# Tying the modulation products and the scan's result transposes to the program's order in a two-block network

## The chip, the cores and the metric

The kernel runs on one core of one Trainium2 chip. Its time is the device time of one execution in microseconds; the time shown for a kernel is the median of several executions. The trace belongs to one further execution, taken with the hardware profiler.

TensorE (PE in the profile; its weight loads are PEld) does the matrix products, VectorE (DVE), ScalarE (ACT) and GpSimd (POOL) the elementwise work, and SyncE's queue (SP) issues the DMA transfers. Each engine works through its own list of instructions in order; semaphores hold an instruction until its operands are there.

## The reference

Two blocks of two layers each, on 256 positions ("lat") and 256 context positions ("ctx") of width 2048, all in fp32. The layers are sliding-window attention, latent attention (mla), a layer with a pooling half and a recurrent half (RWKV), and grouped attention. Ahead of each layer the inputs are modulated by vectors that come from a condition and a large weight matrix (2048 x 6144 per layer). Cut to the modulation and the recurrent half of the third layer:

```python
shift_l, scale_l, gate_l = split(silu(c) @ mod_w[l] + mod_b[l], 3)
shift_c, scale_c, gate_c = split(silu(c_ctx) @ mod_w[l] + mod_b[l], 3)
hl, hc = xl * (1 + scale_l) + shift_l, xc * (1 + scale_c) + shift_c
...
def step(S, xs):                    # per head, along the sequence, both directions
    r, w, k, v, a, b = xs
    sa = einsum('bhvk,bhk->bhv', S, a)
    S = S * w + outer(sa, b) + outer(v, k)
    return S, einsum('bhvk,bhk->bhv', S, r)
...
yn = ((y - mean(y)) * rsqrt(var(y) + GN_EPS)) * gn_g + gn_b
out = (concat([pool(al), yn + bonus]) * silu(gate)) @ ev_w_out
```

## The kernel before

**Products and weights.** All weights come from device memory as fp32 and are used once. `weights` issues the DMA into a tile `raw` on SyncE's queue; `split` turns it into a high part `whi` (ScalarE, L339) and a low part `wlo` (VectorE, L340), so each block of a projection is three products on TensorE (L368 to L370, output `a`). After each block `fill` runs so many steps of side work as the stage's rate says.

**Stages.** First projections (to 157 us of the trace), sliding-window attention (to 705), first out projection (to 885), mla (to 1320), second out projection (to 1450), the third layer with pooling and recurrence (to 2605), third out projection (to 2780), grouped attention and its out projection.

**Modulation.** `mod_steps` is a generator of side work: each step takes one loaded tile `mraw` (1 MB, 192 loads in all; some are halves of another layout, `mod_h`) and issues its matrix products `mv` (L270), four to a step, side by side in four column groups, at the end of which the result is turned and added to `mod`. `PACE` gives the steps per block of weights for each stage: 0.3, 0.5, 0.2, 0, 0.25, 0.5 for the two attention stages, the out projections and the third layer, in the order of the program; the first projections run at rate 0 and demand their groups by `need`. `mod_open` gives a stage buffers for `mraw`, and `mod_close` uses up what is loaded. In the second out projection the rate is 0, but `mod_open` with three buffers lets one load go out.

**Order.** The code is traced, and a scheduler then places the instructions of each engine by priority and by a model of when operands are ready. So an instruction may stand earlier or later on its engine than the code issued it. `keep_in_program_order` ties an instruction behind the one that the code issued just before it on the same engine. Before the change, the second to fourth product of a modulation step are tied; the first, raised in priority, goes where the scheduler's model has it ready.

**The scan.** The recurrence is done in 16 units (8 groups of heads by two directions), each in eight steps. A step is four or five products into a tile `chain` (L1434, L1438, L1444, L1448, L1457) that hang on each other through copies: `Rp` (VectorE, L1437), `SV` (VectorE and ScalarE, L1445, L1446, L1454), `y` (ScalarE, L1460). After the last step y is normalized (VectorE L1465 to L1476, with a Square on ScalarE and a power on GpSimd), and turned by eight transposes `yt` in two banks of four (L1487). Beside a unit's steps the next unit's inputs are made ready: small triangular inversions (`inv`, `z`, `x`, `Z`; L1396 to L1420), Gram matrices (`gram`, L1286), and the projections of the layer itself go on as products `a`.

## Time and profile before

| what | value |
|---|---|
| median of 3 executions | 3263.63 us (3262.27 to 3267.89) |
| profiled execution | 3252.14 us, its span 3250.0 us |
| mean granted TensorE clock (1 is 2.4 GHz) | 0.981 |
| TensorE products / weight loads busy | 95% / 74% of the span |
| VectorE / ScalarE / GpSimd busy | 65% / 46% / 11% |
| read from device memory | 517.46 MB, 170 GB/s with the writes |

The busy share of TensorE counts pipelined products from start to modelled end; the granted clock says in which of two levels the engine ran, 1.00 (2.4 GHz) or 0.50 (1.2 GHz). The profiled execution is shorter than the three that were timed.

### The profile page before, as it was taken

The numbers are of one execution on the slowest core, as the hardware profiler recorded it, in microseconds if no ns is written. First come the engines' busy times: TensorE is split into PE (matmuls) and PEld (weight loads), VectorE is DVE, ScalarE is ACT, GpSimd is POOL, SyncE is SP. The second block draws the span as 40 slices with busy tenths as digits, with TensorE's granted clock in tenths as the row PEclk, the third lists the DMA queues.
The fourth block names the chain that finished last, engine by engine and source line by source line (L and its number), as shares of the span: only waits on it lengthen the run. The fifth ranks groups of instructions, "written<-read, shape, count | busy, mean of one in ns | idle before, by whom it ended". The sixth has DMA issues, their size and how long they took to land. (4 is left out here: it accounts for less than half of the span.)

```text
span 3250.0 us, 53765 instructions
## 1 busy us (share of the span) xinstructions
PE 3080.6 (95%) x20018; PEld 2399.4 (74%) x20018; DVE 2101.4 (65%) x4663; ACT 1481.1 (46%) x3237; POOL 347.7 (11%) x536
## 2 busy tenths in 40 slices
PE   6999999989988999999999999999999999899997
PEld 4667777767777878897776666766767768678887
DVE  3356455543476666665887788778877555857766
ACT  3324444442376666653334333433434424646664
POOL 0000000000001111000122222222221101200000
PEclk8999999999999999999999999999999999999999
DMA  8843444358654656766434434334445474443454
GB/s 309 319 158 130 149 139 153 137 185 283 232 168 136 229 195 230 258 224 204 142 95 150 127 110 133 98 105 148 124 130 161 165 269 141 161 143 130 143 180 152
DMA packets 270773, 556.10 MB, mean 171 GB/s; under 512 B 122928, under 2 KB 150704, under 8 KB 244912
## 3 DMA queue, kind: packets, MB, share of 16 engines
q1 hardware_dynamic: 270512, 552.68, 51.0%
q8 instruction: 157, 2.57, 0.3%
q14 instruction: 104, 0.85, 0.1%
HBM read 517.46 MB, written 35.13 MB: 170 GB/s over the span
## 5 line engine op out<-in xcount | busy, mean ns | idle before, releaser
L340 DVE TENSOR_TENSOR wlo<-raw,whi 128x512 fp32r<-128x512 f32 (+2 forms) x1000 | 660.5, 668 | 545.7 <-ACT whi L339 510.8
L368 PE MATMUL a<-hhi,whi 128*128 128x512 f32 (+1 forms) x2752 | 972.4, 354 | 16.6 <-ACT whi L339 12.1
L339 ACT CAST whi<-raw 128x512 fp32r<-128x512 f32 (+2 forms) x1000 | 592.7, 599 | 800.9 <-PE a L369 467.5
L369 PE MATMUL a<-hlo,whi 128*128 128x512 f32 (+1 forms) x2752 | 947.2, 345 | 0.3 <-DVE hlo L461 0.3
L370 PE MATMUL a<-hhi,wlo 128*128 128x512 f32 (+1 forms) x2752 | 939.8, 347 | 3.4 <-DVE wlo L340 3.1
L368 PEld LDWEIGHTS a<-hhi,whi 128*128 128x128 f32 x2752 | 524.9, 191 | 124.1 <-ACT whi L339 43.3
L370 PEld LDWEIGHTS a<-hhi,wlo 128*128 128x128 f32 x2752 | 522.1, 191 | 61.7 <-DVE wlo L340 8.4
L369 PEld LDWEIGHTS a<-hlo,whi 128*128 128x128 f32 x2752 | 525.6, 191 | 48.7 <-issue 4.5
L472 POOL TENSOR_TENSOR rs<-st,mhalf 128x4 f32<-128x4 f32 (+3 forms) x109 | 149.0, 1367 | 1660.8 <-DVE st L469 1632.9
L368 PE MATMUL a<-whi,hhi 128*128 128x512 f32 (+1 forms) x672 | 262.3, 401 | 15.9 <-ACT sq L629 6.4
L369 PE MATMUL a<-wlo,hhi 128*128 128x512 f32 (+1 forms) x672 | 264.6, 394 | 1.5 <-DVE wlo L340 1.3
L370 PE MATMUL a<-whi,hlo 128*128 128x512 f32 (+1 forms) x672 | 261.2, 391 | 0.0
L270 PE MATMUL mv<-mraw,cs 128*32 128x512 f32 (+1 forms) x1792 | 212.3, 562 | 16.2 <-DMA mraw<-mod_w 10.9
L1443 POOL TENSOR_SCALAR SD<-SV,DL 64x64 f32<-64x64 f32 x224 | 123.8, 553 | 462.5 <-DVE SV L1454 446.2
L368 PEld LDWEIGHTS a<-whi,hhi 128*128 128x128 f32 x672 | 127.1, 191 | 61.5 <-ACT whi L339 12.8
L369 PEld LDWEIGHTS a<-wlo,hhi 128*128 128x128 f32 x672 | 128.9, 192 | 33.7 <-DVE wlo L340 7.7
L370 PEld LDWEIGHTS a<-whi,hlo 128*128 128x128 f32 x672 | 128.5, 191 | 27.5 <-issue 2.9
L581 ACT ACTIVATE pr<-sc,nm 128x512 f32<-128x512 f32 (+1 forms) x128 | 81.0, 633 | 91.9 <-DVE nm L578 66.4
L1437 DVE COPY Rp<-chain 64x64 f32<-64x64 f32 x256 | 56.7, 221 | 72.1 <-PE chain L1434 69.1
L572 DVE TENSOR_REDUCE mx<-sc 128x1 f32<-128x512 f32 (+1 forms) x128 | 78.9, 617 | 37.1 <-PE sc L782 16.1
L1460 ACT COPY y<-chain 64x64 f32<-64x64 f32 x256 | 52.7, 206 | 109.1 <-PE chain L1457 98.4
L1446 ACT COPY SV<-chain 64x64 f32<-64x64 f32 x128 | 26.5, 207 | 161.5 <-DVE SV L1445 153.5
(379 smaller groups left out, 4678.9 us busy)
## 6 DMA issues: line engine op xcount, KB each, us to landing
mraw<-mod_w SPq DMA_DIRECT2D x160, 1024.0 KB, 4.9
raw<-od_in SPq DMA_DIRECT2D x88, 512.0 KB, 3.6
raw<-swa_in SPq DMA_DIRECT2D x72, 512.0 KB, 3.5
mraw<-mod_h SPq DMA_DIRECT2D x32, 1024.0 KB, 6.1
raw<-ev_rkv SPq DMA_DIRECT2D x64, 384.0 KB, 4.0
raw<-ev_in SPq DMA_DIRECT2D x48, 512.0 KB, 4.0
raw<-swa_out SPq DMA_DIRECT2D x40, 512.0 KB, 5.6
raw<-ev_out SPq DMA_DIRECT2D x40, 512.0 KB, 3.7
```

Source lines behind the costliest of these rows:

```text
L270: mm = nc.tensor.matmul(pb[32 * j : 32 * j + 32, :cols], cs[:, 32 * k + 30 - 2 * n : 32 * k + 62 - 2 * n], raw[:, kk, :], start=(n == 0 an ...
L339: nc.scalar.copy(whi, raw)
L340: nc.vector.tensor_tensor(wlo, raw, whi.bitcast(F32), op=ALU.subtract)
L368: mm(out, ah, bh, start=first, stop=False, skip_group_check=shared)
L369: mm(out, ah, bl, start=False, stop=False, skip_group_check=shared)
L370: mm(out, al, bh, start=False, stop=last, skip_group_check=shared)
L472: self.nc.gpsimd.tensor_tensor(dst, stv, mv, op=ALU.pow)
L572: nc.vector.reduce_max(mx, sc, axis=AX.X)
L581: nc.scalar.activation(pr[:, :n], sc, AF.Exp, scale=scale, bias=nm, accum_out=sm)
L1437: nc.vector.tensor_copy(Rp[half[hh]], blk(0, hh))
L1443: nc.gpsimd.tensor_scalar(SD[r_], SV[r_, hh, c, :], DL[r_, c : c + 1], None, ALU.mult)
L1460: nc.scalar.copy(y[r_, c, :], blk(3 * P, hh))
```

## The change

Three edits. In `mod_steps` the first product of a step is tied to the program's order too wherever the stage's rate is above 0 (`paced`). In `rwkv` the first transpose of each bank of four is tied. In the second out projection `mod_open` and `mod_close` are gone, so that this stage has no `mraw` buffers, and the one load that it issued is issued in the next stage.

```diff
--- before.py
+++ after.py
@@ -264,6 +264,7 @@
                             self.mod_load()
                         raw = self.mod_ahead.pop(0)
 
+                        paced = "mod" in self.side and self.side["mod"][1] > 0
                         for kk in range(nk):
                             k, j = nk * q + kk, kk % 4
                             with self.tc.high_priority(None if kk else 0):
@@ -272,7 +273,7 @@
                                     raw[:, kk, :], start=(n == 0 and k < 4), stop=(n == len(gs) - 1 and k >= KD - 4),
                                     tile_position=(0, 32 * j),
                                 )
-                                if kk:
+                                if kk or paced:
                                     self.tc.keep_in_program_order(mm)
                         self.mod_wait = MOD_LAG
                         yield
@@ -1484,7 +1485,9 @@
             for n in range(4):
                 c = 2 * n + c0
                 src = y[:, c : c + 2, :].rearrange("p c t -> p (c t)") if c < NCH - 1 else yw
-                nc.tensor.transpose(pb[:, n * P : (n + 1) * P], src, self.ident)
+                tr = nc.tensor.transpose(pb[:, n * P : (n + 1) * P], src, self.ident)
+                if not n:
+                    self.tc.keep_in_program_order(tr)
             pv = pb.rearrange("p (n t) -> p n t", n=4)
             for hh in range(2):
                 r_, src = half[hh], pv[half[hh], :, hh * L : (hh + 1) * L]
@@ -1818,7 +1821,6 @@
     with tc.tile_pool(name="x2", bufs=1) as px:
         xn = px.tile([P, KD, NT], F32, name="x2")
         N.more(px, XX[1], RX[3])
-        N.mod_open(px, 3, PACE[3])
         N.need(1, range(12))
         w = I["mla_out"]
 
@@ -1847,7 +1849,6 @@
         N.mm_feat(I["ev_lora"][0], h, KD, 256, CTX, [b[:, CTX] for b in lb])
         N.before = None
         N.mm_feat(I["ev_lora"][0], h, KD, 256, LAT, [b[:, LAT] for b in lb])
-        N.mod_close()
         N.dump("x2", xn)
         for k4 in range(0, KD, 4):
             nc.sync.dma_start(out=scratch[:, k4 : k4 + 4, :], in_=xn[:, k4 : k4 + 4, :])
```

Both programs hold the same instructions on every engine; only their order differs. Line numbers behind the edits are higher by one to three in the program after.

**TensorE at the transposes of unit 4's result** (a count behind a row is that of like instructions in a run). `z` and `inv` are the next unit's inversion, `mv` a modulation step, `yt` the transposes of `y`, `a` projection products. Before:

```order
L1407 MATMUL z_4098_19165<-T_4083_19078,NT_18628 32x32 x16
L1396 MATMUL inv_19184<-t_4060_18990,Z_4082_19077 64x64 x16
L270 MATMUL mv_17510<-mraw_19600,cs_9552 32x512 x4
L1487 MATMUL yt_19244<-ident,y_18627 128x128 x4
L1487 MATMUL yt_19251<-ident,y_18627 128x128 x3
L1487 MATMUL yt_19251<-ident,ends_19162 128x128
L270 MATMUL mv_17510<-mraw_19799,cs_9552 32x512 x4
L1420 MATMUL x_4115_19260<-tt,Z_4097_19164 32x32 x16
```

After:

```order
L1408 MATMUL z_4097_19159<-T_4082_19072,NT_18622 32x32 x16
L1397 MATMUL inv_19178<-t_4059_18984,Z_4081_19071 64x64 x16
L370 MATMUL a_19212<-hlo,whi_19217 128x512
L371 MATMUL a_19212<-hhi,wlo_19218 128x512
L369 MATMUL a_19213<-hhi,whi_19217 128x512
L370 MATMUL a_19213<-hlo,whi_19217 128x512
L371 MATMUL a_19213<-hhi,wlo_19218 128x512
L369 MATMUL a_19214<-hhi,whi_19217 128x512
L370 MATMUL a_19214<-hlo,whi_19217 128x512
L371 MATMUL a_19214<-hhi,wlo_19218 128x512
L271 MATMUL mv_17743<-mraw_19112,cs_9552 32x512 x4
L1488 MATMUL yt_19238<-ident,y_18621 128x128 x4
```

Between the last inversion and the transposes stood one modulation step alone; now eight projection products stand there too, and the modulation step is that of another load.

**SyncE's queue at the start of the second out projection.** `raw` are the weights of this projection, `yk` its operand, `x` the context part, `mraw` the modulation load. Before:

```order
L525 DMA yk_13332<-oscr 128x256
L525 DMA yk_13371<-oscr 128x256
L246 DMA mraw_13284<-mod_w 128x2048
L354 DMA raw_13294<-mla_out 128x1024
L1829 DMA x_13236<-ctx 128x4x256
L525 DMA yk_13375<-oscr 128x256
L354 DMA raw_13379<-mla_out 128x1024
```

After:

```order
L526 DMA yk_13330<-oscr 128x256
L526 DMA yk_13369<-oscr 128x256
L355 DMA raw_13292<-mla_out 128x1024
L1831 DMA x_13236<-ctx 128x4x256
L526 DMA yk_13373<-oscr 128x256
L355 DMA raw_13377<-mla_out 128x1024
L526 DMA yk_13411<-oscr 128x256
```

The modulation load has gone from between the operand and the weights.

**TensorE in one step of unit 10.** L1438 and L1444 (L1439 and L1445 after) are the second and third product of a scan step, L1448 (L1449) the fourth; the step's first product, L1434, stands ten rows above the first row here, with projection products between. Before:

```order
L370 MATMUL a_22846<-hhi,wlo_23027 128x512
L1181 MATMUL pool_22833<-pm_22811,pwt_22831 128x512
L1181 MATMUL pool_22839<-pm_22811,pwt_22831 128x512
L1438 MATMUL chain_22625<-SV_22119,AQ_21689 128x128
L1444 MATMUL chain_22625<-Rp_22929,tt 128x64
L368 MATMUL a_22847<-hhi,whi_23026 128x512
L369 MATMUL a_22847<-hlo,whi_23026 128x512
L370 MATMUL a_22847<-hhi,wlo_23027 128x512
L368 MATMUL a_22845<-hhi,whi_23089 128x512
L369 MATMUL a_22845<-hlo,whi_23089 128x512
L370 MATMUL a_22845<-hhi,wlo_23090 128x512
L1448 MATMUL chain_22625<-SV_22119,BKs_22067 128x128
```

After, from the first product (L1435) on:

```order
L1435 MATMUL chain_22619<-SV_22113,AQ_21683 128x128
L371 MATMUL a_22840<-hhi,wlo_22981 128x512
L369 MATMUL a_22841<-hhi,whi_22980 128x512
L370 MATMUL a_22841<-hlo,whi_22980 128x512
L1439 MATMUL chain_22619<-SV_22113,AQ_21683 128x128
L1445 MATMUL chain_22619<-Rp_22923,tt 128x64
L371 MATMUL a_22841<-hhi,wlo_22981 128x512
L369 MATMUL a_22839<-hhi,whi_23020 128x512
L370 MATMUL a_22839<-hlo,whi_23020 128x512
L1449 MATMUL chain_22619<-SV_22113,BKs_22061 128x128
```

Between the first and the second product three projection products are left of ten and two pooling products (`pool`), between the third and the fourth three of six.

## Rows read from the trace of the kernel before

**Rows 1.** The page, busy time by engine: us, share of the span, instructions.

```profile
PE 3080.6 (95%) x20018; PEld 2399.4 (74%) x20018; DVE 2101.4 (65%) x4663; ACT 1481.1 (46%) x3237; POOL 347.7 (11%) x536
```

**Rows 2.** View of waits of TensorE: us in total, times, longest us.

```profile
PE yt L1487 <- DVE y L1476: 11.1, 4, 4.1
...
PE mv L270 <- DMA mraw<-mod_w: 10.9, 6, 3.7
...
PE mv L270 <- DMA mraw<-mod_h: 4.6, 3, 2.1
...
PE yt L1487 <- ACT Z L1411: 3.8, 3, 1.5
```

**Rows 3.** Groups of instructions on TensorE, 1610 to 2605 us, with idle time before.

```profile
L1438 PE MATMUL chain<-SV,AQ 128*128 128x128 f32 x240 | 54.8, 310 | 5.2 <-DVE Rp L1437 4.4
...
L1434 PE MATMUL chain<-SV,AQ 128*128 128x128 f32 x240 | 54.6, 309 | 4.8 <-ACT y L1460 2.0 <-ACT tt L1424 0.2
...
L1448 PE MATMUL chain<-SV,BKs 128*128 128x128 f32 x210 | 48.9, 315 | 2.4 <-ACT SV L1446 1.9
...
L270 PE MATMUL mv<-mraw,cs 128*32 128x512 f32 x312 | 45.0, 651 | 0.3 <-DMA mraw<-mod_w 0.3
```

**Rows 4.** Windows: length; PE, PEld, DVE, ACT, POOL busy; granted clock; DMA share; GB/s.

```profile
1333.50:1340.30 6.80, 6.23 (x29) 6.23 (x30) 3.79 (x7) 4.00 (x9) 0.00 (x0) 0.50 1.00 341
1818.20:1821.60 3.40, 3.26 (x14) 1.23 (x15) 3.26 (x6) 1.48 (x3) 0.73 (x2) 0.51 0.14 58
1876.20:1883.00 6.80, 3.97 (x16) 1.64 (x16) 5.63 (x9) 2.84 (x6) 1.74 (x3) 0.50 0.27 116
2005.90:2012.70 6.80, 6.80 (x53) 4.10 (x46) 4.62 (x9) 2.47 (x6) 0.55 (x1) 0.50 0.60 177
2128.80:2139.00 10.20, 9.46 (x63) 7.39 (x64) 8.36 (x15) 4.23 (x9) 1.71 (x3) 0.50 0.44 157
2398.40:2401.80 3.40, 3.39 (x29) 1.40 (x23) 3.37 (x7) 0.83 (x2) 0.00 (x0) 0.50 0.33 128
1328.00:1334.00 6.00, 1.41 (x11) 0.29 (x10) 0.97 (x3) 1.35 (x4) 0.00 (x0) 0.95 0.94 345
1610.00:2605.00 995.00, 957.22 (x6953) 695.00 (x6952) 770.48 (x1798) 387.90 (x974) 207.91 (x363) 0.98 0.42 129
```

**Rows 5.** Timeline of TensorE, unit 4: start, us, line, tiles, [idle before <-releaser].

```profile
1867.62 0.49 PE L1457 MATMUL chain<-SV,qb 128*128 128x128 f32 x2
...
1869.45 0.40 PE L369 MATMUL a<-hlo,whi 128*128 128x512 f32 x1
...
1869.69 0.40 PE L368 MATMUL a<-hhi,whi 128*128 128x512 f32 x1
...
1872.89 1.06 PE L270 MATMUL mv<-mraw,cs 128*32 128x512 f32 x8
...
1878.07 1.09 PE L1487 MATMUL yt<-ident,y 128*128 128x128 f32 x4 [4.12 <-DVE y L1476]
```

**Rows 6.** Timeline, start of the second out projection, SyncE queue and TensorE.

```profile
1326.47 0.37 SPq L246 DMA_DIRECT2D mraw<-mod_w  x1
...
1326.89 0.42 SPq L354 DMA_DIRECT2D raw<-mla_out  x1
...
1332.09 1.07 PE L270 MATMUL mv<-mraw,cs 128*32 128x512 f32 x8 [3.74 <-DMA mraw<-mod_w]
...
1334.07 0.58 PE L368 MATMUL a<-hhi,whi 128*128 128x256 f32 x1 [0.92 <-ACT whi L339]
```

**Rows 7.** Timeline of TensorE, start of the scan stage's projections.

```profile
1456.64 1.06 PE L270 MATMUL mv<-mraw,cs 128*32 128x512 f32 x8 [1.41 <-DMA mraw<-mod_w]
```

**Rows 8.** Timeline of TensorE, first out projection.

```profile
714.03 1.06 PE L270 MATMUL mv<-mraw,cs 128*32 128x512 f32 x8 [3.63 <-DMA mraw<-mod_w]
```

**Rows 9.** Timeline of TensorE, two products of one scan step.

```profile
2250.71 0.48 PE L1434 MATMUL chain<-SV,AQ 128*128 128x128 f32 x2
...
2254.06 0.49 PE L1438 MATMUL chain<-SV,AQ 128*128 128x128 f32 x2 [0.78 <-DVE Rp L1437]
```

## The prediction

> **What bounds the kernel now.** The page's busy line comes first: TensorE works 95% of the span [rows 1], 3080.6 of 3250.0 us, so about 170 us of idle time and whatever the engine loses at its lower clock are all that a new order can win; the two programs hold the same instructions, engine by engine. Next I asked the view of waits for the two operations that the change ties down [rows 2]. The transposes of the scan's result waited 11.1 us for VectorE's y in four places and 3.8 us for ScalarE's Z in three, 14.9 us in all. The modulation products waited 10.9 us (six places) and 4.6 us (three) for their own loads. Then the groups of the scan's stretch, 1610 to 2605 us [rows 3]: there the modulation products waited 0.3 us in all, so in the scan the change has nothing to win at them, only at the transposes. Last, the granted clock by stretches [rows 4]: after such waits it stood at 0.50 (1.2 GHz) for five stretches in the scan, 3.4, 6.8, 6.8, 10.2 and 3.4 us, 30.6 us in all.
>
> The kernel's profiled execution took 3252.14 us, 2.14 around its span of 3250.0. The median of the runs shown is 3263.63, 11.5 above it. The sum below is made against 3252.14 and then carried over to the median. A change under 0.2% (6.5 us) can't be told from none.
>
> **The change part by part.**
>
> *Transposes.* A stall of unit 4 is typical [rows 5]. Its last scan product starts at 1867.62 and takes 0.49; a chain of VectorE, ScalarE and GpSimd (mean, square, power, multiplication) then runs until y is ready at 1877.9, 9.8 us later. TensorE had only 60 instructions to do in between, and after the modulation product at 1872.89 it stood for 4.12 us. The order shows why: four transposes stood behind the inversion steps and one modulation product with nothing else. In the changed order eight more projection products stand there. They follow each other by 0.24 us [rows 5], so I count the work from the last scan product to the transposes by such spacings: 5.9 us before, 10.9 us now, over the 9.8 that y needs. The same count for the other three: unit 8, 52 to 74 instructions, 6.8 to 10.9 us; unit 12, 70 to 123, 8.4 to 20.2; unit 3, 67 to 61, 7.7 to 8.6, where some 1.2 us of wait should stay. So about 10 of the 11.1 us should go. Of the 3.8 us behind Z I take 1 us as gone, since Z hangs on a chain of its own. Against it stand units that lose cover: unit 2 goes from 97 to 85 instructions, 12.9 to 9.5 us, which by the 9.8 gives a new wait of under 1 us, and one or two more are near the edge. Together **−9**; bounds 0 (y itself becomes later by as much as the transposes do) and −14.9 (no wait stays).
>
> *The clock in the scan.* Work in a stretch at 1.2 GHz takes twice its time, so the 30.6 us cost up to 15.3 us. Each of the five begins during one of the waits above or within 2 us behind it. If the waits go the clock stays up; but new waits elsewhere can bring it down again, and waits behind Z that stay keep theirs. I take near half, **−7**, bounds 0 and −15.3. The Trainium skill, "TensorE: Matmul & The Clock Gate", Part 1, section "What's actually happening", says that for modelling the ramp penalty is under 1% of a typical span. By it this term would be left out and the sum would be 7 us smaller. The trace agrees with the share (15.3 of 3250 is 0.5%), but here that is over twice what can be told from no change, so the term stays.
>
> *Cover taken from the scan's steps.* The projection products that now stand ahead of the transposes are missing elsewhere. In each of the scan's steps (eight per unit) three products hang on each other through copies on VectorE and ScalarE; what stands between them on TensorE hides these copies. So far the three waited 12.4 us in the whole stretch [rows 3]. One such step shows the price: from the first product to the second, 3.35 us passed with 0.78 of it idle, for the copy Rp [rows 9]. In unit 10 the order shows a step of which ten projection products and two pooling products stood between the first and the second product, and now only three products, 0.7 us of work. I counted all steps in this way, work between products against the time that their operands took to come: 3 us lacked before, 23 us lack now, 8 of them in unit 10. That is the upper bound, +20; the lower is 0, since these operands came so late because VectorE and ScalarE had other things in front, which moved too. I take **+7**, nearer the lower end, since in most steps the missing piece is under half a microsecond.
>
> *The second out projection.* Its one modulation load, 1 MB, is issued at 1326.47, ahead of 512 KB of the projection's own weights at 1326.89 [rows 6]. DMA moved 345 GB/s at a share of 0.94 until 1334 [rows 4], so 1 MB is 3 us of the queue. TensorE stood 3.74 us for the product and then 0.92 us for the weights behind it. Without the load the weights should be there about 3 us earlier; the product itself (1.07 us) is done in the next stage, and what is taken from that queue is only worth its time until the next wait for weights, where DMA is the limit through the first groups. **−2**; bounds 0 (DMA is late at the next weights anyway) and −8 (4.66 us of waits and half of the 6.8 us at 1.2 GHz that followed at 1333.5 [rows 4]). In the first projection of the scan's stage a modulation product at 1456.64 waited 1.41 us for its load [rows 7]; it now stands 29 instructions later, behind products that ended after 1464 in the trace: **−1.4**.
>
> *First and third out projection, both attention stages.* The longest wait for a modulation load there, 3.63 us at 714.03 [rows 8], is that of a product which keeps its place; the next one moves 24 instructions back, but the products ahead of which it stood wait for weights that SyncE issues behind the same load. In the first attention stage 18 of 38 modulation products move back by 13 to 57 instructions, in the mla stage most by one place or none; neither stage loses or gains cover that the trace shows to be scarce. **0**, bounds −3 and +3.
>
> Sum: −9 −7 +7 −2 −1.4 = −12.4. 3252.1 becomes 3239.7, and the median 3263.6 becomes **3251**.
>
> **The rivals.**
>
> *VectorE sets the end of the scan.* It is busy 770.5 of 995 us there, 77% [rows 4]; TensorE's weight loads only 695.0. If the scan's chains of VectorE work follow each other without slack, the stretch ends when they do, and a transpose that no longer waits only moves the wait to the next product. Then only the second out projection and 1456 stay, −3.4: 3260, not to be told from before. For it: the wait's releaser is VectorE in 11.1 of 14.9 us. Against it: 23% of VectorE's time was free. The Trainium skill, "Perfetto Trace Analysis", section "Identifying the Most-Contended Engine", says that TensorE's headroom is judged by the busy share of its weight loads and not of its products, and by it VectorE is the scan's most contended engine. To the same time leads that the tie does not do what it says: a transpose is tied only to the TensorE instruction that the code issued just before it, and where that one floats forward the transpose may follow it; the order around unit 4 speaks against that.
>
> *Everything comes back.* The waits of the transposes go altogether (−14.9), the clock stays up (−15.3), the steps' copies come as much earlier as the cover shrinks (0 to +4), and the second out projection gives 3.4: about −30, 3233. For it: five stretches at 1.2 GHz that all follow these waits. Against it: unit 3's count, and Z.
>
> *The lost cover costs more than the stalls did* (slower). The place is the scan's steps, unit 10 above all, around 2232 us. If the 20 us that lack by the count are all waited for, and the new waits bring the clock down as often as the old ones did (term 0), the sum is −9 +20 −3.4 = +7.6: 3271. It decides from the point where the three step products wait some 19 us more than the 12.4 of before. For it: the copies between steps are on the path of every unit, and a wait there recurs eight times a unit. Against it: the new holes are short, while the old ones of 4 us were long enough to be followed by 1.2 GHz.
>
> **How the numbers follow.** The forecast, 7 to 20 us faster, gets 0.42 (3244 to 3257 is its own range); everything comes back 0.16; VectorE sets the end 0.24; lost cover 0.18. So faster by over 0.2% is 0.58, within 0.2% 0.24, slower 0.18. The range has to reach to both outer cases to leave out no more than 2 in 10: 3231 (just under the case at 3233) to 3272 (just over the one at 3271).
>
> **What would show it.** In the changed profile, the transposes' idle time for y should fall from 11.1 to some 2 us, and the stretches at 0.50 near 1818, 1876 and 2129 should be gone; if those at 2005 and 2398 remain, Z holds them. The step products' idle time should rise from 12.4 to about 19. The product at 1332 should be missing, and the first weights of the second out projection come 3 us earlier. The prediction is wrong if the step products' waits rise by over 19 us, if y's end moves along with the transposes, or if the scan's stretch keeps its 995 us though the transposes do not wait.

## The result, and the profile after

| | before | after |
|---|---|---|
| median of the timed executions | 3265.76 us (4) | 3299.56 us (4; 3296.13 to 3309.65) |
| profiled execution, span | 3252.14, 3250.0 us | 3296.13, 3294.0 us |
| mean granted clock | 0.981 | 0.976 |

The ratio is 1.011, 95% interval [1.0093, 1.0128]: the change made the kernel slower by 30 to 42 us. The forecast was 3251, with a range of 3231 to 3272. In one of the six executions of the run only_x2, below, the granted clock was 0.693 and the time 3976.84 us; it is left out of that run's figures.

The page's busy line answers to [rows 1]. TensorE's busy time is longer by 11 us for the same instructions, and its share of the span is lower:

```profile
PE 3091.8 (94%) x20018; PEld 2409.7 (73%) x20018; DVE 2104.8 (64%) x4663; ACT 1481.1 (45%) x3237; POOL 354.7 (11%) x536
```

The view of waits of TensorE, after, answers to [rows 2]. The transposes' waits for y and Z are down from 14.9 to 2.9 us, as forecast. A group that stood at 3.1 us before, the third products of a projection waiting for `wlo`, is now the longest of all (`g`, L562, is VectorE's read of a finished projection; AQ is an operand of the Gram matrices):

```profile
PE a L371 <- DVE wlo L341: 33.1, 12, 8.7
...
PE mv L271 <- DMA mraw<-mod_h: 7.3, 5, 2.9
...
PE mv L271 <- DMA mraw<-mod_w: 6.2, 6, 3.7
...
PE a L369 <- DVE g L562: 3.8, 1, 3.8
...
PE gram L1287 <- DVE AQ L1294: 3.5, 3, 1.2
...
PE yt L1488 <- ACT Z L1412: 1.8, 2, 0.9
...
PE yt L1488 <- DVE y L1477: 1.1, 1, 1.1
```

The groups of the scan's stretch, after (1610 to 2644 us), answer to [rows 3] (the third number group is idle time before the instructions and what ended it). The three scan products named there wait 13.7 us in all where they waited 12.4; the forecast was 19. Of the 33.1 us of waits for `wlo`, 30.2 stand in this stretch:

```profile
L371 PE MATMUL a<-hhi,wlo 128*128 128x512 f32 x679 | 280.8, 425 | 30.2 <-DVE wlo L341 30.2
...
L1435 PE MATMUL chain<-SV,AQ 128*128 128x128 f32 x240 | 56.2, 316 | 8.8 <-ACT y L1461 4.8 <-ACT tt L1425 0.6
...
L1439 PE MATMUL chain<-SV,AQ 128*128 128x128 f32 x240 | 55.2, 313 | 3.7 <-DVE Rp L1438 3.2
...
L271 PE MATMUL mv<-mraw,cs 128*32 128x512 f32 x312 | 43.3, 628 | 0.0
...
L1449 PE MATMUL chain<-SV,BKs 128*128 128x128 f32 x210 | 48.8, 314 | 1.2 <-ACT SV L1447 0.8
```

From the first transpose of unit 0 to the last of unit 15 the kernel before takes 964.1 us (windows: length, PE busy, PEld, DVE, ACT, POOL, granted clock):

```profile
1616.10:2580.20 964.10, 926.32 (x6762) 670.60 (x6759) 756.45 (x1776) 377.32 (x956) 205.28 (x362) 0.98 0.42 130
```

The same stretch after, and a piece of it in unit 3:

```profile
1614.80:2618.90 1004.10, 939.28 (x6762) 682.60 (x6759) 758.66 (x1776) 377.40 (x956) 212.91 (x362) 0.96 0.41 124
1815.60:1825.80 10.20, 3.40 (x11) 1.03 (x11) 8.07 (x14) 0.88 (x2) 1.31 (x5) 0.52 0.16 41
```

It is 40.0 us longer, 91% of the 44.0 us by which the span grew. TensorE is idle for 64.8 us in it (length less busy), where it was idle for 37.8: +27.0. Its busy time grew by 13.0 us, which the clock, longer at 1.2 GHz, can account for. Added up over 200 equal windows of some 5 us as length times (1 less granted clock), 20.4 us were lost to the lower clock before and 39.3 are lost after. (Part of the loss falls on idle time, which is why its growth, 18.9, is more than the 13.0 of busy time.) Ahead of it the kernel after is 4.3 us behind at the first weights of the first out projection (707 us of before), but that is back by the first transposes, which start at 1614.8, 1.3 us earlier than before. The remaining 5 us stand in the third out projection, behind the scan. The 44.0 us are those of one execution each; between the medians it is 33.8.

Unit 3 shows one of the two longest of the new waits. Timeline of TensorE, after, from the end of unit 3's last scan product on (start, length, line, tiles, [idle before <-releaser]):

```profile
1807.55 0.67 PE L1397 MATMUL inv<-Z,t 64*64 64x64 f32 x14
...
1811.45 0.39 PE L370 MATMUL a<-hlo,whi 128*128 128x512 f32 x1
...
1812.65 1.15 PE L1397 MATMUL inv<-t,Z 64*64 64x64 f32 x32
...
1822.40 1.65 PE L371 MATMUL a<-hhi,wlo 128*128 128x512 f32 x3 [8.60 <-DVE wlo L341]
...
1823.98 1.94 PE L271 MATMUL mv<-mraw,cs 128*32 128x512 f32 x8
...
1825.84 0.47 PE L1488 MATMUL yt<-ident,y 128*128 128x128 f32 x1
```

VectorE in the same piece:

```profile
1815.99 0.69 DVE L1477 TENSOR_TENSOR y<-y,rs 128x512 f32<-128x512 f32 x1
...
1819.86 0.69 DVE L1146 TENSOR_TENSOR df<-vp 128x512 f32<-128x512 f32 x1
...
1821.13 0.74 DVE L1147 SCALAR_TENSOR_TENSOR v<-df,vec,vp 128x512 f32<-128x512 f32 x1
...
1821.80 1.49 DVE L341 TENSOR_TENSOR wlo<-raw,whi 128x384 fp32r<-128x384 f32 x3
```

ScalarE had made the last of the three `whi` that these subtractions need 11 us earlier:

```profile
1810.34 0.51 ACT L340 CAST whi<-raw 128x384 fp32r<-128x384 f32 x1 [1.31 <-issue]
```

y was ready at 1816.7. The transposes started at 1825.8: they stood behind a modulation step, and that behind a third product whose `wlo` VectorE makes at 1821.8, after y, after the copy for Z, the two operations for tt and five more operations for the next unit, without a pause between them. So it is VectorE's order that holds `wlo` back here, and not its load from memory or `whi`. TensorE waited 8.60 us, and the granted clock of that piece is 0.52. Before, the wait at this place was for y, and it was 2.09 us:

```profile
1818.28 1.09 PE L1487 MATMUL yt<-ident,y 128*128 128x128 f32 x4 [2.09 <-DVE y L1476]
```

### The profile page after: what moved, and what is told of

The parts are those of the page before. It is cut to its first block, busy times and chain, and to the rows that moved or that the text cites. A ratio compares the mean times of both kernels' runs of the same rounds, so it can differ in the third digit from the quotient of the medians.

```text
span 3294.0 us, 53793 instructions
## 1 busy us (share of the span) xinstructions
PE 3091.8 (94%) x20018; PEld 2409.7 (73%) x20018; DVE 2104.8 (64%) x4663; ACT 1481.1 (45%) x3237; POOL 354.7 (11%) x536
## 5 line engine op out<-in xcount | busy, mean ns | idle before, releaser
L371 PE MATMUL a<-hhi,wlo 128*128 128x512 f32 (+1 forms) x2752 | 947.2, 349 | 33.3 <-DVE wlo L341 33.1
L271 PE MATMUL mv<-mraw,cs 128*32 128x512 f32 (+1 forms) x1792 | 209.9, 556 | 13.6 <-DMA mraw<-mod_h 7.3
L1444 POOL TENSOR_SCALAR SD<-SV,DL 64x64 f32<-64x64 f32 x224 | 127.2, 568 | 508.7 <-DVE SV L1455 492.5
L1438 DVE COPY Rp<-chain 64x64 f32<-64x64 f32 x256 | 56.6, 221 | 71.8 <-PE chain L1435 68.7
```

The costliest lines, as they stand in the source:

```text
L271: mm = nc.tensor.matmul(pb[32 * j : 32 * j + 32, :cols], cs[:, 32 * k + 30 - 2 * n : 32 * k + 62 - 2 * n], raw[:, kk, :], start=(n == 0 an ...
L371: mm(out, al, bh, start=False, stop=last, skip_group_check=shared)
L1438: nc.vector.tensor_copy(Rp[half[hh]], blk(0, hh))
L1444: nc.gpsimd.tensor_scalar(SD[r_], SV[r_, hh, c, :], DL[r_, c : c + 1], None, ALU.mult)
```

## The experiments

All were run on the chip with the kernel before beside them. The table gives the ratio of times with its interval, the difference of medians, and for the stretch from the first to the last transpose of the scan its length, TensorE's idle time and the time lost to the lower clock, all from the profile and worked out as above. The last column is not from the profile: the span and the mean granted clock of every execution are known, and span times (1 less clock) is what one execution loses to the lower clock in the whole program. Shown is the difference of its median against that of the kernel before beside it, good to some 2 us, since the clocks have three places. For the kernel after it is a span, against before beside each of the others.

| run | ratio [95%] | median, us | scan, us | idle | lost to clock | lost, all executions |
|---|---|---|---|---|---|---|
| before | | | 964.1 | 37.8 | 20.4 |  |
| only_yt | 0.9999 [0.9988, 1.0010] | −1.6 | 966.0 | 38.1 | 22.2 | −3 |
| only_x2 | 0.9956 [0.9940, 0.9972] | −15.7 | 960.4 | 34.6 | 12.0 | −17 |
| yt_x2 | 0.9978 [0.9968, 0.9988] | −9.2 | 965.1 | 34.7 | 17.0 | −10 |
| ties_not_scan | 0.9986 [0.9975, 0.9996] | −3.2 | 967.8 | 34.1 | 20.5 | −13 |
| wlo_50_before | 0.9996 [0.9981, 1.0010] | −1.2 | 968.7 | 34.2 | 22.2 | 0 |
| tie_one | 1.0014 [1.0002, 1.0026] | +1.2 | 967.8 | 38.4 | 23.8 | +7 |
| tie_first_half | 1.0035 [1.0019, 1.0050] | +12.6 | 984.2 | 38.8 | 42.7 | +13 |
| tie_second_half | 1.0049 [1.0033, 1.0065] | +13.4 | 981.8 | 50.4 | 29.0 | +10 |
| only_mod | 1.0077 [1.0062, 1.0091] | +23.8 | 988.9 | 47.9 | 41.0 | +17 |
| mod_scan_only | 1.0088 [1.0073, 1.0104] | +28.2 | 986.8 | 50.0 | 37.5 | +17 |
| mod_x2 | 1.0096 [1.0080, 1.0112] | +28.6 | 996.4 | 48.7 | 49.4 | +25 |
| after | 1.0110 [1.0093, 1.0128] | +33.8 | 1004.1 | 64.8 | 39.3 | +12 to +16 |
| mod_yt | 1.0148 [1.0135, 1.0161] | +49.8 | 1010.0 | 65.9 | 44.4 | +24 |
| wlo_50 | 1.0100 [1.0082, 1.0118] | +31.3 | 998.4 | 48.0 | 39.2 | +14 |
| wlo_first | 1.0133 [1.0118, 1.0148] | +43.3 | 1004.6 | 57.2 | 35.9 | +12 |
| wlo_first_before | 1.0102 [1.0085, 1.0118] | +30.4 | 1001.3 | 50.9 | 32.4 | +4 |
| filler | 1.0104 [1.0091, 1.0117] | +31.1 | 997.7 | 46.3 | 22.2 | +1 |

Scan less lost to clock splits the loss in the scan, roughly, since part of the lower clock falls on idle time: 943.7 us before, 947 to 949 with the modulation steps of the scan or of the whole program tied, 965 and 966 with the transposes tied too (after, mod_yt). The rest of each loss in the scan is the clock.

**The three edits apart.** First theory (A): the two ties together put products that need a late `wlo` ahead of the transposes. The count of such products in each kernel's order (third products between a unit's last scan product and its transposes, whose `wlo` stands on VectorE behind y's last operation) is 37 in eight units after, and none before but four in unit 14. Each of the first runs keeps one or two hunks of the diff shown above: only_yt the transposes' hunk, only_mod the two hunks in `mod_steps`, mod_yt these and the transposes', only_x2 the last two.

> Only the transposes of the scan's result are tied; modulation products and the second out projection as before. In this order no third product of a projection (hhi with wlo) whose wlo stands on VectorE behind y stands ahead of the transposes, except four in one unit, as before. Theory A (the two ties together put such products ahead of the transposes, and TensorE stands for wlo behind y's chain): about no change, -6 to +4 us, waits for wlo near the 3.1 us of before. Rival B (the transposes' tie takes cover from the scan's steps): slower by 10 to 25 us. Rival C (the modulation tie alone costs it): no change.

> Only the modulation products are tied. Seven third products with a late wlo stand ahead of the transposes, all in unit 10. Theory A: slower by 5 to 15 us, from a wait for wlo in unit 10 (near 2289 us in the kernel after) and the clock behind it; no such wait in units 3, 5, 6, 12. Rival B: -3 to +3. Rival C: slower by 30 us or more.

> Both ties, the second out projection as before. Late third products ahead of the transposes in units 3, 5, 6, 8, 9, 10, 12 (3, 4, 3, 4, 4, 7, 8). Theory A: slower by 28 to 42 us, waits for wlo of 25 us or more in these units. Rival B and C: the sum of the two single runs. If the second out projection's edit had a part in it, clearly less than the kernel after's 34.

> Only the modulation buffers of the second out projection are gone. All theories: 0 to -4 us, the wait at 1332 us gone and its load issued in the next stage; the forecast's term was -2.

The tie of the transposes alone costs nothing. The tie of the modulation steps alone costs 24 us, where theory A gave 5 to 15 for the one unit with late products. Both together cost 50, more than their sum and more than theory A's 28 to 42. The edit in the second out projection gains 16 us in the timed executions. Its place in the trace shows 3 us of it. The first weights behind the load that is gone, 1334.07 before [rows 6], in only_x2 and then after:

```profile
1333.64 0.39 PE L368 MATMUL a<-hhi,whi 128*128 128x256 f32 x1 [2.96 <-ACT whi L339]
```

```profile
1332.57 0.58 PE L369 MATMUL a<-hhi,whi 128*128 128x256 f32 x1 [3.21 <-ACT whi L340]
```

They come 0.4 and 1.5 us earlier by the clock of the trace. But the projection products just ahead of them come 2.3 and 1.0 us later than before (at 1328.98 and 1327.65, against 1326.64), so against these the weights are 2.8 and 2.5 us earlier, near the 3 forecast. The wait for weights takes the place of the one for the load. In the profile the whole span of only_x2 is 3249.8 us, that of before 3250.0. The rest of the gain is the clock: in the five executions the granted clock was 0.980 to 0.986, where before had a median of 0.979, and by the last column they lose 17 us less to it. The same holds for yt_x2, which loses 10 us less and is 9 us faster. Where in the program the clock stays up is not known, since one execution of only_x2 was profiled, and it is the second slowest of the five.

**Where the modulation tie costs.** The next runs tie only outside the scan (with the other two edits), or only in it:

```diff
+                        paced = "mod" in self.side and self.side["mod"][1] not in (0, PACE[4])    # ties_not_scan
+                        paced = "mod" in self.side and self.side["mod"][1] == PACE[4]             # mod_scan_only
```

> The kernel after, but the modulation products of the scan's stage are not tied (those of the other stages, the transposes and the second out projection as after). Four late products in one unit by the order. Theory A: the loss in the scan is gone: -14 to 0 us against the kernel before, of it some -13 from the second out projection and up to +7 from the first attention stage, where the traces with tied modulation products were 6 to 8 us behind by 400 us. Rival: if the ties outside the scan carried the loss, it stays above +15.

> Only the modulation products of the scan's stage are tied, all else as before. Seven late products in unit 10 by the order. Theory A: +10 to +20 us: the 8.7 us wait of unit 10 and what the clock loses behind it, without the 6 to 8 us of the first attention stage that the run only_mod shows by 400 us. Rival B: +3 or less.

Without the ties in the scan the loss is gone; with these ties alone it is there, 28 us. Theory A asked for 10 to 20. The waits for `wlo` in mod_scan_only are those of one unit:

```profile
PE a L371 <- DVE wlo L341: 11.8, 7, 8.7
```

That leaves more than half of the loss to something else, and the table says what: the time lost to the lower clock went from 20 to 37 us, though one long wait alone was added. Over all executions it grew by 17 us too.

**Taking the late products away.** Raising the subtraction that makes `wlo` on VectorE, in the scan's stage, in the kernel after and in the kernel before as a control:

```diff
-        nc.vector.tensor_tensor(wlo, raw, whi.bitcast(F32), op=ALU.subtract)
+        with self.tc.high_priority(50 if getattr(self, "hot", False) else 0):      # wlo_first: None, ahead of all
+            nc.vector.tensor_tensor(wlo, raw, whi.bitcast(F32), op=ALU.subtract)
```

> The kernel after, with the subtraction that makes wlo placed ahead of all other VectorE work in the scan's stage (highest priority in the scheduler). By the order no third product with a wlo behind y is left ahead of the transposes in any unit (0 of 16; the kernel after has 37 such products in eight units). Theory A (TensorE stands for wlo behind y's chain): the long waits for wlo (8.6, 6.5, 8.7 us) are gone, their total is below 8 us, and the time falls by 25 us or more against the kernel after, to 3250 to 3275. Rival B (lost cover in the scan's steps, lost by the tie itself): stays within 10 us of the kernel after.

> The kernel before with the same priority for wlo in the scan's stage, a control for the run wlo_first. Theory A: no long waits for wlo were there to be taken away, so little changes: -8 to +6 us. If it gains as much as wlo_first does against the kernel after, then wlo first is a gain by itself and proves nothing of the ties.

> The kernel after, with the subtraction that makes wlo raised by only 50 places of priority in the scan's stage (the run wlo_first put it ahead of everything and delayed y's chain too). By the order six late third products are left ahead of the transposes, three each in units 10 and 12, instead of 37 in eight units. Theory A: the waits for wlo fall from 33.1 us to under 15, and the time by 10 to 30 us against the kernel after, to 3270 to 3290; the stalls of units 3 and 6 are gone. Rival B (the loss is in the steps' lost cover): within 8 us of the kernel after.

> The kernel before with the same 50 places, the control. Theory A: nothing to take away, so -6 to +12 us. If it gains 10 us or more, the gain of wlo_50 is not one of the late products.

wlo_first missed: 3306 us where theory A gave 3250 to 3275. It proves little, since its control loses 30 us by itself: y's chain and the other chains now stand behind `wlo`. wlo_50 has a control that changes nothing, and it splits theory A. The view of waits of wlo_50 (line numbers are higher by one or two):

```profile
PE a L372 <- DVE wlo L342: 7.6, 6, 4.5
...
PE yt L1490 <- DVE y L1479: 6.3, 3, 3.0
```

The waits for `wlo` fell from 33.1 to 7.6 us, and the idle time of the scan from 64.8 to 48.0. So the late products do make the waits. But wlo_50 is 31.3 us slower than before, where the kernel after was 33.8: a fall of 2.5 us, with intervals that overlap, where 10 to 30 were expected. TensorE's busy time in the scan rose from 939 to 950 us:

```profile
1620.70:2619.10 998.40, 950.41 (x6761) 687.66 (x6758) 757.35 (x1776) 378.93 (x956) 210.09 (x362) 0.96 0.41 125
```

The time lost to the lower clock is the same as in the kernel after (39.2 and 39.3 us), so the clock is not what lengthened the busy time; what did was not found. By the wording of its expectation the result is that of rival B (within 8 us of the kernel after), yet B's mechanism does not show: the three products of a scan step wait 12.4 us in wlo_50, just as before the change. So the price of the late products in time is not shown: taking 25 us of their waits away gave next to nothing back.

mod_x2 and yt_x2 complete the set:

> The kernel after without the tie of the transposes. Theory A: the late products of unit 10 alone are left (7 of them), so +8 to +16 us against before (the 24 of only_mod less the 13 of only_x2), which is some 20 us faster than the kernel after. Were the edits simply additive, it would be within 4 us of the kernel after, since the tie alone cost nothing (only_yt).

> The kernel after without the tie of the modulation products. Four late products in unit 13. If the gain of the run only_x2 is real and the tie of the transposes by itself costs nothing: -8 to -16 us against before. If only_x2's gain was chance of its order: -5 to +5.

mod_x2 missed (+29, not +8 to +16): the last edit, which takes 16 us off the kernel before and 16 off mod_yt, takes nothing off only_mod (+5, with intervals that overlap). By the last column the clock is 25 of its 29. yt_x2 came within its bounds at −9. Both kernels without a modulation tie but with the last edit are faster than the kernel before: only_x2 is the fastest version measured.

**The clock.** But for the run filler, below, every kernel with the steps of the whole scan tied loses 36 to 49 us to the lower clock there; every one with none of them tied, or one, loses 12 to 24 (wlo_first_before, with its own stalls, 32). Second theory (D): before, the modulation steps and some projection products filled the stretch behind the transposes, where the next unit's small products wait for copies; tied, they go earlier with the projection, and this stretch is left bare. In the orders, 184 projection products and 8 modulation steps stand between the transposes and the last Gram matrices, summed over the units, in the kernel before; 163 and 8 in mod_scan_only, 145 and 1 in the kernel after.

```diff
+                        paced = step == 143                          # tie_one; step counts the modulation steps
+                        paced = 143 <= step <= 160                   # tie_first_half
+                        paced = 161 <= step <= 180                   # tie_second_half
...
             pbs = [self.bank("gram") for _ in range(2)]
+            for hh in range(2):                                      # filler, on mod_scan_only
+                for _ in range(2):
+                    mm(pbs[hh], self.h[0][:, 0, 0:P], self.h[0][:, 1, :], start=True, stop=True)
```

> The kernel before with one single modulation step tied, the one that stood behind the transposes of unit 0 (at 1622 us, between a scan product and the Gram matrices). Theory D: at that place a wait of about 1 us for AQ and a stretch at 1.2 GHz appear (before: 0.19 us and none), 3 to 6 us lost by the middle of unit 1; what the rest of the order does to the total is open: -4 to +10 us. If the step's place does not matter: unit 1 starts within 1.5 us of before.

The place in the kernel before, timeline of TensorE and the window from the step on:

```profile
1622.03 0.49 PE L1434 MATMUL chain<-SV,AQ 128*128 128x128 f32 x2 [0.22 <-ACT tt L1424]
1622.44 1.06 PE L270 MATMUL mv<-mraw,cs 128*32 128x512 f32 x8
1623.70 1.13 PE L1286 MATMUL gram<-AQ,BK 64*128 64x128 f32 x8 [0.19 <-DVE AQ L1293]
```

```profile
1622.40:1630.40 8.00, 7.56 (x47) 5.54 (x46) 7.16 (x19) 0.71 (x3) 0.87 (x2) 1.00 0.59 176
```

In tie_one, with the one step tied, its timeline and the windows before and behind 1624 us:

```profile
1622.78 0.49 PE L1437 MATMUL chain<-SV,AQ 128*128 128x128 f32 x2 [0.21 <-ACT tt L1427]
1624.45 1.13 PE L1289 MATMUL gram<-AQ,BK 64*128 64x128 f32 x8 [1.18 <-DVE AQ L1296]
1625.82 1.62 PE L1289 MATMUL gram<-AQ,BK 64*128 64x128 f32 x6 [0.25 <-DVE AQ L1296]
```

```profile
1616.00:1624.00 8.00, 6.93 (x74) 5.01 (x73) 7.82 (x14) 3.60 (x8) 1.88 (x3) 1.00 0.67 215
1624.00:1632.00 8.00, 7.30 (x27) 6.03 (x28) 5.05 (x13) 1.23 (x3) 0.00 (x0) 0.61 0.28 83
```

The step had stood in the hole in which the Gram matrices wait for AQ. With it gone they wait 1.18 us instead of 0.19, and the clock, at 1.00 until then, falls to a mean of 0.61 over the next 8 us, where it was 1.00 before. The rows around are the same otherwise. The other engines' operations near 1620 us come 0.8 us later than before, those near 1632 us 4.5: within the 3 to 6 us that theory D gave. One execution could be chance: at unit 3, where before and only_yt have the same order, a wait of 0.83 us for AQ has the clock at 1.00 behind it in before, and one of 0.90 in only_yt has 0.53. But the other traces agree at this place. The six other kernels that tie this step and have nothing else there (tie_first_half, only_mod, mod_scan_only, mod_x2, mod_yt, after) all wait 1.18 us for AQ, and over the 8 us from the first Gram product on their clock is 0.69 to 0.84 (tie_one: 0.82). In before, only_yt, only_x2, yt_x2, ties_not_scan and tie_second_half, which do not tie it, it is 1.00; in filler and wlo_50 the step is tied, but no such wait arises, and it is 1.00 too. The total of tie_one is hardly told from none (interval up to +0.26%).

In the kernel after this place is one of three of its kind. The scan has nine stretches at 0.50, 78 us together. Three, 27 us, begin in the long waits for `wlo` of units 3, 6 and 10. Three more begin during the waits of 1.18 us for AQ behind the transposes of units 0, 4 and 11:

```profile
1621.40:1631.60 10.20, 9.41 (x32) 8.01 (x33) 6.24 (x16) 1.01 (x3) 0.44 (x1) 0.50 0.33 86
...
1891.00:1897.80 6.80, 5.81 (x23) 5.11 (x23) 4.62 (x12) 0.41 (x1) 0.00 (x0) 0.50 0.36 106
...
2368.90:2382.60 13.70, 12.17 (x42) 9.79 (x43) 8.89 (x23) 1.86 (x6) 1.61 (x3) 0.50 0.29 66
```

These are 30.7 us, at half clock a loss of 15. Of the other three, two begin in the wait for g in unit 12 and just behind a wait of 1.96 us of a scan step, and one, at 2085.6, behind no wait over 1 us.

> Only the modulation steps of the first half of the scan (units 0 to 7) are tied. No late third product ahead of the transposes. Theory D: +6 to +14 us, all of it lost by 2100 us of the trace, and the lost time at 1.2 GHz raised by some 8 to 12 us there; from 2150 on as before. Theory A alone: 0.

> Only the modulation steps of the second half (units 8 to 15) are tied. Seven late third products in unit 10. As before until 2200 us; then the 8.7 us wait for wlo in unit 10 and 1.2 GHz behind it: +12 to +20 us. With tie_first_half it should add up to the +28 of mod_scan_only.

```profile
1615.90:2600.10 984.20, 945.45 (x6762) 688.48 (x6758) 757.79 (x1776) 378.42 (x956) 207.33 (x362) 0.96 0.41 127
```

The first half, with no late product beyond those of before and no wait over 3.1 us in the scan, has the idle time of before (38.8 us against 37.8), is 20 us longer in the scan and loses 22 us more to the clock. This profile is the slowest of its eight executions, so the size is overstated (8 to 12 us were expected). But over all executions 13 us more are lost to the clock, and the time is 12.6 us longer: there the clock is the whole of the loss. It also limits theory D: 183 projection products and 7 steps stand behind its transposes, nearly the number of before, so it is not their sum that decides; that it is which hole stays bare fits, but no count of holes was made that foretells it. The second half has the 8.7 us wait in unit 10 and 9 us of lost clock. The two add up to 26 us, mod_scan_only's 28.

> The kernel of the run mod_scan_only with 128 extra products (128x512, their result overwritten by the Gram matrices that follow in the same banks) between the transposes and the Gram matrices, eight per unit, 30 us of TensorE work by their spacing of 0.24 us. Theory D (the tied modulation steps leave the stretch behind the transposes bare: TensorE idles there for copies and its clock falls): the time lost at 1.2 GHz in the scan falls from 37.5 us toward the 20 of before, and the time rises by much less than the 30 us of added work, by 0 to 15 us over mod_scan_only. If the clock's loss has another cause (the long wait in unit 10, say): loss at 1.2 GHz within 5 us of 37.5, time +25 us or more over mod_scan_only.

The groups of Gram matrices in mod_scan_only and in filler (its rows with hhi are the added products):

```profile
L1287 PE MATMUL gram<-AQ,BK 64*128 64x128 f32 x448 | 62.5, 328 | 3.9 <-DVE AQ L1294 3.5 <-ACT yf L1497 0.4
```

```profile
L1290 PE MATMUL gram<-AQ,BK 64*128 64x128 f32 x448 | 56.1, 300 | 0.0
...
L1285 PE MATMUL gram<-hhi 128*128 128x512 f32 x112 | 42.2, 465 | 0.2 <-ACT yf L1500 0.2
```

And the scan's windows of the two:

```profile
1617.50:2604.30 986.80, 936.81 (x6762) 682.34 (x6759) 757.41 (x1776) 378.08 (x956) 210.07 (x362) 0.96 0.42 127
```

```profile
1619.70:2617.40 997.70, 951.43 (x6875) 684.39 (x6871) 761.04 (x1775) 378.25 (x956) 206.35 (x361) 0.98 0.41 125
```

The 128 added products are 30 us of work by their spacing and cost 3 us over mod_scan_only (31.1 against 28.2). The Gram matrices' waits went from 3.9 us to none, the granted clock from 0.96 to 0.98, the loss to the clock from 37.5 to 22.2 us. Over all executions filler loses no more to the clock than the kernel before (+1 us), where mod_scan_only loses 17 more. The added products also moved others, so not all of it need be theirs, but work that does nothing paid nearly for itself.

## Why the prediction was wrong

The change was forecast to gain 12 us and cost 34, more than the slowest rival gave (lost cover, 3271).

*Transposes, −9: right at its own place.* Their waits fell by 12.0 us, and unit 4, on which the count was shown, no longer waits. *The step that failed is the count of cover.* It took every projection product that stands ahead of the transposes as work that is ready. Of these, every third needs `wlo`, and `wlo` stands on VectorE's list behind y's own chain. Where such products stood ahead, the transposes came later, not earlier. From a unit's last scan product to its transposes, traces before and after:

| unit | late products ahead | before, us | after, us |
|---|---|---|---|
| 1 | 4 | 13.2 | 16.6 |
| 3 | 3 | 9.9 | 18.7 |
| 5 | 4 | 12.8 | 17.7 |
| 6 | 3 | 9.7 | 18.7 |
| 9 | 4 | 13.1 | 16.9 |
| 10 | 7 | 12.6 | 25.5 |
| 12 | 8 | 9.6 | 25.1 |
| 13 | 4 | 13.6 | 16.6 |
| the other eight, mean | 0 (unit 14: 4, before too) | 10.9 | 10.5 |

The eight with late products grew by 61 us together; the scan grew by 40, so some 20 came back elsewhere, which fits work done early that is then missing behind the transposes. In the trace after, y of these eight units had been ready for 5.7 to 14.2 us when the transposes started. Unit 12, with the most, shows no wait for `wlo`: there a first product waits 3.78 us for g, which stands behind y on VectorE too. So the error is wider than `wlo`: a product counted as cover must have all that it waits for. The forecast had unit 3 down for 1.2 us of wait and unit 12 for none. It looked at the four units that waited before, and for each at the length of the queue in front, not at what that queue waits for. The missing term is the waits for `wlo`: +30 us of idle time in the profile, where all idle time of the scan grew by 27.0. What it is worth in time is open, since wlo_50 took most of it away for 2.5 us.

*The clock, −7: wrong in sign.* It measured +19 in the profiles (20.4 to 39.3 us lost), +12 to +16 over all executions. The prediction tied the clock to the waits at the transposes and counted five stretches at 0.50 in the scan before, 30.6 us. There are seven, 40.8 us; in the 9 us ahead of the two left out no wait is over 0.8 us:

```profile
1729.40:1732.80 3.40, 3.40 (x11) 2.75 (x10) 2.47 (x9) 1.51 (x3) 1.66 (x1) 0.50 0.88 332
2074.20:2081.00 6.80, 6.67 (x25) 4.86 (x23) 4.84 (x14) 0.79 (x2) 0.84 (x2) 0.50 0.17 36
```

So the trace before already said that the clock falls without a long wait. tie_one and tie_first_half show it falling behind waits of 1 us, where the small products behind the transposes are left without dense ones between. The Trainium skill, "TensorE: Matmul & The Clock Gate", Part 1, "What's actually happening", puts the ramp under 1% of a typical span for modelling. Here the clock falls again and again, and the loss in the scan alone is 39.3 of 3294 us, 1.2%; that figure is no bound for this kernel's loss.

*Cover taken from the scan's steps, +7.* Measured +1.3 (12.4 to 13.7 us). The bound of +20 was far off; that the operands moved with the products would explain it, but was not followed up. Rival "lost cover" had the right sign for another reason: cover was lost, but behind the transposes, not between the scan's steps.

*Second out projection, −2; 1456, −1.4.* The product at 1332 is gone and the one at 1456 no longer waits, and against the products ahead of them the first weights came 2.5 us earlier, near the 3 forecast. So the term was right at its place. The timed gain of −16 with this edit alone is outside the term's range of 0 to −8: the prediction gave the edit no part in the clock of the rest of the program, and 17 us less are lost to it.

*Rival "VectorE sets the end"* said that a wait moves to the next product. That is what happened in units 3, 6 and 10, but VectorE was not full (758.7 of 1004.1 us): it is the order on it, not its load. *First and third out projection and attention, 0:* at the first weights of the first out projection the kernel after was 4.3 us behind and only_mod 6.8, against −0.5 in mod_scan_only, so in these profiles the ties in the first attention stage cost more than the ±3 given; but in the kernel after the stages up to the scan gave it back.

Shown by runs: the scan is the place, the tied modulation steps are the cause, the clock is the whole of the loss in the half where no late product is added, and late products make the waits for `wlo`. Open: what these waits cost in time, after wlo_50; what makes up the 18 us, besides the clock, that the transposes' tie adds in the scan to the modulation tie; and why the clock falls at the other places of the scan. tie_one shows one hole and filler that dense work there keeps the clock up, but no count of the order foretells the loss. Only argued: that the transposes' tie stretches the modulation tie (each is tied to what stands in front of it, so a transpose behind a tied step stands behind every product ahead of that step); the counts agree (none with the transposes tied alone, seven in unit 10 with the steps tied alone, 37 with both and the last edit), but no run broke that link by itself.

## What to carry to other kernels

Work that stands ahead of a waiting instruction covers the wait only if its own operands come earlier: follow each operand to its place on the engine that makes it before counting it. A small independent product that a scheduler floats into the holes of a dependent chain can be worth more than its own time, where it keeps the clock up; tying it to the program's order can take it out of the holes. Ties need not add: here two together cost more than their sum, so try each tie alone and both together. And read the granted clock of every execution, not of the profiled one alone: it told where the gain of only_x2 came from.

## What the runs showed that was not expected

A single modulation step of 1.06 us, moved away from behind unit 0's transposes, brought a stretch at 1.2 GHz with only 1.18 us of idle time ahead of it. And 128 useless products of 0.24 us each made the scan's clock rise from 0.96 to 0.98 and cost 3 us of their 30. An edit of one load in the second out projection gained 16 us, about as much as the clock gave back, and nothing beside the modulation tie alone (mod_x2). A kernel's profiled execution lies up to 14 us below and up to 5 us above its median here (before: 3252.1 against 3265.8; yt_x2: 3257.4 against 3252.1), so a few microseconds between two profiles say nothing by themselves; the timed medians decide.
